# First stage of a hybrid attention and convolution backbone: x and context loaded feature-major, the row factor applied when products leave PSUM, and attention values computed with tokens on partitions and kept in DRAM

## The chip, the cores and the metric

The kernel runs on one core of a Trainium2 chip. The metric is the device time of one execution in microseconds. Five engines work side by side, each on its own list of instructions: TensorE (PE) multiplies matrices into PSUM, VectorE (DVE), ScalarE (ACT) and GpSimd (POOL) work element by element, and SyncE (SP) mostly issues DMA transfers. An instruction that needs another engine's result waits on a semaphore, and everything behind it on its engine waits with it.

## What is computed

Two layers over 1024 latent tokens of 1024 features, with a context of 256 tokens. The change touches the first layer's input side:

```python
h_lat = rmsnorm(x, norm_g[0]) * (1 + scale) + shift       # scale, shift from c
h_ctx = rmsnorm(ctx, norm_g[0]) * (1 + scale_c) + shift_c # from c_ctx
...
proj = h_lat @ w_in
q = apply_rope(split_heads(proj[..., :q_end], N_Q_HEADS), cos, sin)
k = apply_rope(split_heads(proj[..., q_end:k_end], N_KV_HEADS), cos, sin)
v = split_heads(proj[..., k_end:v_end], N_KV_HEADS)
z = proj[..., v_end:]
...
kv_c = h_ctx @ w_in[:, q_end:v_end]
kc = split_heads(kv_c[..., :KV_WIDTH], N_KV_HEADS)
vc = split_heads(kv_c[..., KV_WIDTH:], N_KV_HEADS)
...
o = windowed_attention(q, k, v, kc, vc, sink)
y = (o * jax.nn.silu(z)) @ w_out
```

There are 16 query heads in 4 groups, each group with one key and one value head of 128. A query sees a window of 384 latent keys and all 256 context keys. The second layer is a gated convolution; nothing of it changes.

## The kernel before

Every fp32 operand is split into a high and a low part (fp32r), and each product of matrices is done as three: high by high, low by high, high by low. In the names the high part of the features is `hh` (`Hh`), the low part `hl` (`Hl`); for weights `whi` and `wlo`. Features stand on partitions in eight tiles (kt 0 to 7) of 1024 tokens. The splits of one tile are an ACT copy and a DVE or POOL subtraction.

*First stage.* The rows of x come with tokens on partitions (`xs0`, four tiles for tokens 0 to 511). ACT sums their squares, DVE makes the row factor, and PE turns the rows: the first ten by a product with a diagonal of factors (`dg`), the others by transposes of rows already scaled (`turn_scaled` at L455, `turn`, `turn_apart`). ACT and DVE then add scale and shift (`x_tile`). The modulation itself is made column block by column block: `ada_mm` (L400) multiplies silu(c) and silu(c_ctx) by the modulation weights, 32 columns at a time on four quarters of the array, and `ada_cols` turns the rows to columns. K, Q and V of group 0 and head 0 are accumulated over the eight tiles for the first 512 tokens (`x_mm`, L502, with `acc0`), and then for the other 512 (`acc1`), whose x comes feature-major from the host (`k_xt`) and is multiplied by a broadcast of the row factor (`rb1`). Context tiles (`c_tile`, L492) are turned on PE in between. V is computed feature-major like K; `vt_split` (L628) turns it with PE transposes of `vf` and splits it. `spin` is a product on zeros that keeps PE running.

*Attention.* A loop runs over 16 heads and 8 query blocks of 128. Each step issues the next block's scores, then `fill(FILL)` (L1319) takes 12 products (15 in a few steps) from a queue of projections that later heads need (q, z), then a product with values (`pv`, twice or so per head), then the transposes of the probabilities that DVE, ACT and POOL made meanwhile. At a change of group ("regroup") the key job and the value job (`job`, L1056) of the next group run whole. Weights come in a stream of 40 chunks (`wsA`), the first four split with DVE and the others with POOL.

PE's list is kept in program order (`pin("P")`); in the first stage DVE's and ACT's as well. Otherwise a scheduler orders DVE, ACT and POOL, with `tc.high_priority` and `after` (an order without a wait) as hints. SP issues all loads in order, each gated by one some eight loads earlier.

## Time and profile before

| | us |
|---|---|
| median of three runs | 1678.78 (1678.36 to 1679.4) |
| profiled execution | 1678.26 |
| its span | 1676.5 |
| PE busy | 1665.9 |
| DVE, ACT, POOL busy | 1116.2, 879.7, 868.1 |
| first product on x starts | 16.04 |
| first transposes of probabilities start | 82.7 |

The span runs from the first to the last instruction. "Busy" counts the time in which at least one instruction of the engine runs. The recorded duration of a product includes its way through the array, and products overlap: one with 512 columns is recorded with some 390 ns, while the next starts after 227. Steps are therefore read from start to start. The first stage ends and the attention begins around 70 to 80 us.

### The profile page before, as it was taken

The page shows a single profiled execution, that of the slowest core. Times are in us where ns is not written, and L with a number is a line of the kernel's source. Part 1 is how long each engine was busy: PE and PEld are TensorE (multiplying, and loading weights), DVE is VectorE, ACT ScalarE, POOL GpSimd, SP SyncE. Part 2 cuts the span into 40 slices and gives each one's busy share as a digit, 9 for nine tenths or more (in the row PEclk, how much of TensorE's full clock was granted, in tenths as well). Part 3 has the DMA queues.
Part 4 walks back from the last instruction along what each step waited for, and adds up shares of the span by engine and source line. Part 5 has one row for each costly group of instructions (what it writes and reads, how often), then busy time and mean ns, then how long its engine had stood idle before and what let it go on. Part 6 is the DMA issues. An engine that isn't in the chain of part 4 may idle for free.

```text
span 1676.5 us, 23887 instructions
## 1 busy us (share of the span) xinstructions
PE 1665.9 (99%) x8414; PEld 1409.6 (84%) x8414; DVE 1116.2 (67%) x2121; ACT 879.7 (52%) x1555; POOL 868.1 (52%) x720
## 2 busy tenths in 40 slices
PE   9999999999999999999999999999999999999998
PEld 6888888888888888888888888888888888888886
DVE  5755644556366645566234399999999999868732
ACT  6745544555355544555333365655656664556741
POOL 0256653666366663642001267999898887130400
PEclk9999999999999999999999999999999999999999
DMA  9434433545254443447976523020211212377881
GB/s 377 162 88 151 144 113 101 151 154 145 77 154 154 144 131 93 139 148 276 310 246 210 200 88 101 0 78 16 71 51 51 89 38 70 132 271 253 308 298 50
DMA packets 114935, 244.54 MB, mean 146 GB/s; under 512 B 11768, under 2 KB 36736, under 8 KB 114816
## 3 DMA queue, kind: packets, MB, share of 16 engines
q1 hardware_dynamic: 108736, 233.06, 41.3%
q10 hardware_dynamic: 6080, 9.97, 2.4%
q8 instruction: 66, 1.08, 0.3%
q14 instruction: 53, 0.43, 0.1%
HBM read 190.80 MB, written 41.69 MB: 139 GB/s over the span
## 4 chain that ended last, share of the span: by engine, by line
PE 98%; DMA 1%; DVE 0%; POOL 0%; SPq 0%; ACT 0%; issue 0%
PE psg L89 51%; PE pss L89 26%; PE pso L89 21%; DMA wraw_page<-in_k_win_dram 1%; SPq L89 0%; POOL rope_half L89 0%; DVE x_page L89 0%; POOL ql_page L89 0%; POOL low_page L89 0%; DVE wlo_page L89 0%; ACT whi_page L89 0%; DVE ptlo L89 0%; POOL p_page L89 0%; ACT pthi L89 0%; DVE hf_page L89 0%
## 5 line engine op out<-in xcount | busy, mean ns | idle before, releaser
L89 POOL TENSOR_TENSOR odd_half<-odd_half,prod_half 128x513 f32<-128x513 f32 (+2 forms) x252 | 314.4, 1256 | 24.4 <-ACT prod_half L89 10.8
L89 POOL TENSOR_TENSOR wlo_page<-wraw_page,whi_page 128x512 fp32r<-128x512 f32 (+1 forms) x104 | 172.0, 1669 | 181.8 <-DVE ql_page L89 71.6
L89 PE MATMUL psg<-hh_page,whi_page 128*128 128x512 f32 x600 | 236.2, 394 | 0.0
L89 PE MATMUL psg<-hl_page,whi_page 128*128 128x512 f32 x600 | 234.4, 391 | 0.0
L89 PE MATMUL psg<-hh_page,wlo_page 128*128 128x512 f32 x600 | 234.3, 390 | 0.0
L89 ACT ACTIVATE prod_half<-ubuf,dww 128x513 f32<-128x513 f32 (+2 forms) x252 | 165.7, 675 | 117.0 <-POOL odd_half L89 113.0
L89 PE MATMUL psg<-h2h_page,whi_page 128*128 128x512 f32 x464 | 181.9, 392 | 0.0
L89 PE MATMUL psg<-h2h_page,wlo_page 128*128 128x512 f32 x464 | 180.6, 389 | 0.0
L89 PE MATMUL psg<-h2l_page,whi_page 128*128 128x512 f32 x464 | 180.5, 389 | 0.0
L89 POOL TENSOR_SCALAR p_page<-p_page,sc 128x640 f32<-128x640 f32 (+1 forms) x128 | 99.7, 779 | 153.7 <-DVE sc L89 131.6
L89 DVE SCALAR_TENSOR_TENSOR pss<-ubuf,dww,pss 128x512 f32<-128x512 f32 (+3 forms) x270 | 172.9, 674 | 0.1
L89 DVE SCALAR_TENSOR_TENSOR pss<-ubuf,wsum,pss 128x512 f32<-128x512 f32 (+3 forms) x270 | 172.2, 674 | 0.2
L89 ACT ACTIVATE p_page<-p_page,sc 128x641 f32<-128x641 f32 (+1 forms) x128 | 103.1, 805 | 101.9 <-DVE sc L89 99.3
L89 DVE TENSOR_TENSOR ptlo<-pss,pthi 128x512 fp32r<-128x512 f32 (+2 forms) x144 | 102.0, 717 | 67.1 <-ACT pthi L89 66.0
L89 ACT ACTIVATE pthi<-pss 128x512 fp32r<-128x512 f32 (+2 forms) x144 | 87.4, 618 | 105.3 <-PE pss L89 99.4
L89 PEld LDWEIGHTS psg<-hh_page,wlo_page 128*128 128x128 f32 x600 | 112.7, 188 | 24.4
L89 PEld LDWEIGHTS psg<-hh_page,whi_page 128*128 128x128 f32 x600 | 112.7, 188 | 19.1 <-ACT hh_page L89 0.3
L89 PEld LDWEIGHTS psg<-hl_page,whi_page 128*128 128x128 f32 x600 | 112.8, 188 | 18.4
L89 ACT ACTIVATE whi_page<-wraw_page 128x1024 fp32r<-128x1024 f32 x88 | 92.6, 1053 | 51.6 <-PE psg L89 20.6
L89 PE MATMUL pso<-h2h_page,whi_page 128*128 128x512 f32 x304 | 118.3, 389 | 0.0
L89 PE MATMUL pso<-h2l_page,whi_page 128*128 128x512 f32 x304 | 118.3, 389 | 0.0
L89 PE MATMUL pso<-h2h_page,wlo_page 128*128 128x512 f32 x304 | 118.3, 389 | 0.0
(260 smaller groups left out, 3985.1 us busy)
## 6 DMA issues: line engine op xcount, KB each, us to landing
wraw_page<-in_k_wconv_dram SPq DMA_DIRECT2D x48, 512.0 KB, 3.4
wraw_page<-in_k_win_dram SPq DMA_DIRECT2D x40, 512.0 KB, 3.6
wo_page<-in_attn_w_out_dram SPq DMA_DIRECT2D x32, 512.0 KB, 6.4
wol_page<-wolA SPq DMA_DIRECT2D x32, 512.0 KB, 6.6
wo_page<-in_conv_w_out_dram SPq DMA_DIRECT2D x32, 512.0 KB, 7.0
wol_page<-wolC SPq DMA_DIRECT2D x32, 512.0 KB, 5.6
rope_half<-rope_half ACTq DMA_DIRECT2D x76, 128.0 KB, 2.4
araw_page<-in_k_ada_dram SPq DMA_DIRECT2D x16, 512.0 KB, 10.2
```

Of the source, the lines that this page charges most:

```text
L89: r = f(*a, **k)
```

## The change

x and ctx come from the host feature-major, all tokens (`k_xt`, eight tiles, and `k_ct`, two). A tile is multiplied by its scale column alone and split (`u_tile`: `uh`, `ul`). K and Q of group 0 and head 0, and now also Z of head 0, are accumulated from these for all 1024 tokens; Z runs five tiles late (`ZLAG`). The row factor is put in when the sum leaves PSUM (`scaled`). The sums of squares that it needs are made feature-major: ACT squares, POOL adds, and PE sums over partitions in `roots`; `spread` broadcasts the factor. What the shift adds to each output column is a sum over features of weight times shift: POOL multiplies and adds (`shift_part`), PE sums over partitions, and ACT adds it (`wb`).

The tiles `hh` and `hl` are then made from x, row factor, scale and shift (`h_tile`), and the context's from `ct` (`ctx_tiles`). Values are computed for all four groups at once with tokens on partitions (`v_block`: 24 products of 512 columns for each of 8 latent and 2 context blocks, with weights `wv` from the host), split, written to DRAM (`vd`), and read back for each group (`load_values`). So the value jobs, `vf` and `vt_split` go. K and Q of the first group get their positions on whole pages, with SP swapping the halves.

In the loop the number of fill products is 12, 12, 11, 10 for heads 0 to 3 and then 10 or 11, and 12 in the last head; at a change of group 54 products of the queue stand in place of the value job. `tie` puts POOL's weight splits behind a softmax operation. The stream has 36 chunks, of which DVE splits only the first.

```diff
+ZLAG = 5
+AT_ONCE = (7,)
+FILLED = 7
+PACE = (12, 12, 11, 10)
+POOLED = (2, 5)
...
-    wsA = WStream(chunks, nraw=4, lo_eng=lambda i: V if i < 4 else G)
+    wsA = WStream(chunks, nraw=2, lo_eng=lambda i: G if i else V)
...
+    def u_tile(kt, a, b):
+
+        if kt not in U:
+            U[kt] = pg.alloc(F32R, [1024], "uh"), pg.alloc(F32R, [1024], "ul")
+        h, l = (t[:, a:b] for t in U[kt])
+        g = mods[kt][:, 1, 0:1]
+        act(h, xt[kt][:, a:b], AF.Copy, scale=g)
+        stt(l, xt[kt][:, a:b], g, h.bitcast(F32), ALU.mult, ALU.subtract)
...
+        act(t, xt[kt], AF.Square)
+        tt(G, sqs, sqs, t, ALU.add)
...
+    def roots(sq, n, o):
+
+        for b in range(n):
+            PE.matmul(o[:, b:b + 1], sq[:, b * P:b * P + P], ones[:, 0:1], start=True, stop=True)
...
+    def shift_part(kts):
+
+        for kt in kts:
+            for i, n in enumerate("kqz"):
+                a, w, b = wb_pg[:, i * P:i * P + P], W0[n][0][:, kt], mods[kt][:, 0, 0:1]
+                t = a if kt == 0 else wb_pg[:, 3 * P:4 * P]
+                G.tensor_scalar(out=t, in0=w, scalar1=b, scalar2=1.0, op0=ALU.mult, op1=ALU.mult)
+                if kt:
+                    tt(G, a, a, t, ALU.add)
...
+                stt(f[:, 0:CT], ct[kt // 4][:, kt % 4], m[:, 1, 1:2], rbc, ALU.mult, ALU.mult)
+                act(h, f[:, 0:CT], AF.Identity, bias=m[:, 0, 1:2])
+                ctx_low.append(stt(l, f[:, 0:CT], m[:, 0, 1:2], h.bitcast(F32), ALU.add, ALU.subtract))
...
+            r1 = roots(sqs, 8, ps_o(1))
+            pg.free(sqs)
+            rc = roots(csq[0][:, 0], 2, ps_o(1))
...
+    spread(rc, 2, rbc)
+    for kt in range(ZLAG, KT - 1):
+        x_mm(kt, "z")
+    spread(r1, 8, rb)
+    ctx_tiles(range(KT))
+    x_mm(KT - 1, "z")
...
+        behind_ctx(stt(f, xt[kt], m[:, 1, 0:1], rb, ALU.mult, ALU.mult))
+        act(Hh[kt], f, AF.Identity, bias=m[:, 0, 0:1])
+        if kt in POOLED:
+            act(f, f, AF.Identity, bias=m[:, 0, 0:1])
+            for a in range(0, 1024, 512):
+                split_lo(G, *(t[:, a:a + 512] for t in (Hl[kt], f, Hh[kt])))
+        else:
+            stt(Hl[kt], f, m[:, 0, 0:1], Hh[kt].bitcast(F32), ALU.add, ALU.subtract)
...
+    run(v_block(oc, TB))
+    h_tile(0)
+    h_tile(1)
+    vz = scaled(acc0["z"])
+    oc = ps_o(0)
+    run(v_block(oc, TB + 1))
...
+    V.tensor_copy(wb, o[:, 0:3])
...
     for kt in range(KT):
+        for n in range(4):
+            run(v_mm(accv[n], kt, *v_lhs(kt, n)))
         if kt + 2 < KT:
+            h_tile(kt + 2)
...
+            fill(FILL if h == NH - 1 else PACE[h] if h < 4 else 10 + (qb % 3 == 0))
...
+        if h and h % 4 == 0 and qb == 2:
+            load_values(h // 4)
...
-            run(job(("v", g)))
+            enqueue(("z", nxt[0]))
+            fill(54)
```

PE's first instructions before, behind 32 spins, where `zerr` are the zeros of `spin`, `araw` the modulation weights, and `dg` the diagonal of row factors:

```order
L89 MATMUL pso_233<-araw_page_99,c_page_170 32x256 x4
L89 MATMUL pso_233<-araw_page_100,c_page_170 32x256 x4
L89 MATMUL psg_247<-dg_half_212,x_page_90 128x128
L89 MATMUL psg_247<-dg_half_212,x_page_91 128x128
L89 MATMUL psg_247<-dg_half_212,x_page_92 128x128
L89 MATMUL pso_251<-ident,arow_half_98 128x2 x2
L89 MATMUL psg_247<-dg_half_212,x_page_93 128x128
L89 MATMUL psg_257<-dg_half_212,x_page_90 128x128
L89 MATMUL psg_257<-dg_half_212,x_page_91 128x128
L89 MATMUL psg_257<-dg_half_212,x_page_92 128x128
L89 MATMUL psg_257<-dg_half_212,x_page_93 128x128
L89 MATMUL pss_85<-zerr_page_82 128x512 x2
```

PE's first instructions in the changed kernel:

```order
L94 MATMUL pss_85<-zerr_page_82 128x512 x8
L94 MATMUL pso_171<-araw_page_96,c_page_159 32x128 x8
L94 MATMUL pss_85<-zerr_page_82 128x512 x2
L94 MATMUL pso_184<-ident,arow_half_180 128x2
L94 MATMUL pss_85<-zerr_page_82 128x512 x4
L94 MATMUL pss_168<-uh_page_191,whi_page_195 128x512
L94 MATMUL pss_168<-ul_page_192,whi_page_195 128x512
L94 MATMUL pss_168<-uh_page_191,wlo_page_196 128x512
L94 MATMUL pss_168<-uh_page_191,whi_page_195 128x512
L94 MATMUL pss_168<-ul_page_192,whi_page_195 128x512
L94 MATMUL pss_168<-uh_page_191,wlo_page_196 128x512
```

The turning of x stands no longer ahead of the first products, one modulation block stands there instead of two half blocks of double width, and 14 spins instead of 34.

POOL, whose first instruction of work before is a weight split of the attention, starts in the changed kernel with ten sums of squares (`sqs`, `csq`) and the 45 instructions of `shift_part`, 24 products and 21 sums.

DVE in the changed kernel, where the context tiles are made (`hcf` and `hcl`; `own` are the sums that leave PSUM):

```order
L94 SCALAR_TENSOR_TENSOR hcf_half_696<-ct_page_136,mod,rbc_half_646 128x256
L94 SCALAR_TENSOR_TENSOR hcl_page_677<-hcf_half_682,mod,hch_page_676 128x256
L94 SCALAR_TENSOR_TENSOR hcf_half_704<-ct_page_136,mod,rbc_half_646 128x256
L94 SCALAR_TENSOR_TENSOR hcf_half_708<-ct_page_136,mod,rbc_half_646 128x256
L94 SCALAR_TENSOR_TENSOR hcf_half_700<-ct_page_136,mod,rbc_half_646 128x256
L94 SCALAR_TENSOR_TENSOR hcl_page_695<-hcf_half_696,mod,hch_page_694 128x256
L94 SCALAR_TENSOR_TENSOR hcl_page_695<-hcf_half_704,mod,hch_page_694 128x256
L94 SCALAR_TENSOR_TENSOR hcl_page_695<-hcf_half_708,mod,hch_page_694 128x256
L94 SCALAR_TENSOR_TENSOR hcl_page_695<-hcf_half_700,mod,hch_page_694 128x256
L94 TENSOR_TENSOR own_page_812<-pss_168,rb_page_647 128x512
L94 TENSOR_TENSOR own_page_815<-pss_169,rb_page_647 128x512
L94 TENSOR_TENSOR own_page_812<-pss_168,rb_page_647 128x512
```

Before, `hcl` stood in pairs between the feature tiles of the second 512 tokens:

```order
L89 TENSOR_TENSOR hcl_page_661<-hf_page_665,hch_page_660 128x256
L89 TENSOR_TENSOR hcl_page_661<-hf_page_672,hch_page_660 128x256
L89 SCALAR_TENSOR_TENSOR hl_page_409<-hf_page_651,mod_177,hh_page_408 128x512
L89 SCALAR_TENSOR_TENSOR hf_page_687<-xt_page_162,mod_178,rb_page_514 128x512
L89 TENSOR_TENSOR hcl_page_661<-hf_page_692,hch_page_660 128x256
L89 TENSOR_TENSOR hcl_page_661<-hf_page_699,hch_page_660 128x256
```

The sixteen operations of the context tiles now stand together, ahead of the evacuation of the first products and of all feature tiles.

DVE in the changed kernel, further on: the fourth feature tile's low part is `hl_page_940`:

```order
L94 SCALAR_TENSOR_TENSOR hf_page_959<-xt_page_120,mod,rb_page_647 128x1024
L94 COPY ident<-pso_891 128x3
L94 TENSOR_TENSOR vout_page_887<-pso_862,vout_page_887 128x512
L94 TENSOR_SCALAR pso_1199<-dww_raw,cs 128x256
L94 SCALAR_TENSOR_TENSOR hf_page_941<-xt_page_118,mod,rb_page_647 128x1024
L94 SCALAR_TENSOR_TENSOR hl_page_958<-hf_page_959,mod,hh_page_957 128x1024
L94 SCALAR_TENSOR_TENSOR pso_1199<-ident,abt,pso_1199 128x128
L94 SCALAR_TENSOR_TENSOR hf_page_977<-xt_page_124,mod,rb_page_647 128x1024
L94 SCALAR_TENSOR_TENSOR hf_page_997<-xt_page_130,mod,rb_page_647 128x1024
L94 SCALAR_TENSOR_TENSOR pso_1199<-ident,abt,pso_1199 128x128
L94 TENSOR_TENSOR own_page_812<-own_page_812,cos_page_733 128x1024
L94 SCALAR_TENSOR_TENSOR hl_page_940<-hf_page_941,mod,hh_page_939 128x1024
```

It stands behind the `hf` of three later tiles, the copy of `wb` and the multiplication of K by the cosines.

717 lines of the change are left out of this document (334 added, 383 removed).

## The prediction

> **What bounds the kernel now.** I read the page's busy table and its chain first, then TensorE's waits, the busy times by stretch, and last the timelines of TensorE and of the DVE (VectorE) and POOL (GpSimd) engines.
>
> ```profile
> span 1676.5 us, 23887 instructions
> PE 1665.9 (99%) x8414; PEld 1409.6 (84%) x8414; DVE 1116.2 (67%) x2121; ACT 879.7 (52%) x1555; POOL 868.1 (52%) x720
> PE 98%; DMA 1%; DVE 0%; POOL 0%; SPq 0%; ACT 0%; issue 0%
> PE pss L89 <- DVE zerr_page L89: 2.0, 1, 2.0
> PE pso L89 <- DMA araw_page<-in_k_ada_dram: 0.6, 1, 0.6
> 0.00:20.00 20.00, 17.14 (x101) 12.57 (x101) 7.39 (x22) 14.09 (x22) 1.12 (x7) 1.00 0.89 344
> 20.00:40.00 20.00, 20.00 (x159) 13.25 (x159) 12.65 (x28) 10.75 (x17) 0.00 (x0) 1.00 1.03 408
> ```
>
> PE is busy for 1665.9 of 1676.5 us and is 98% of the chain that ended last; its two longest waits are 2.0 and 0.6 us. So the time is what PE streams, plus its start and end. An edit pays only if it takes work off PE, and it costs only where it makes PE wait. The stretches (span, then PE, PEld, DVE, ACT, POOL busy, clock, DMA) show POOL at work for 1.12 us in the first 20 us and for none in the next 20, while DMA runs at 408 GB/s. That idle POOL is what the change fills.
>
> The profiled execution took 1678.26 us, its span and 1.76 us around it; the median is 1678.78, 0.5 us away. The sum is made against 1678.26.
>
> **PE work that goes.** The step of a product with 512 columns, and the price of a transpose, are read from starts, since durations overlap:
>
> ```profile
> 53.00 0.39 PE L89 MATMUL pss<-hl_page,whi_page 128*128 128x512 f32 x1
> 53.23 0.60 PE L89 MATMUL pso<-ident,x_page 128*128 128x128 f32 x4
> 53.59 0.47 PE L89 MATMUL psg<-hh_page,whi_page 128*128 128x512 f32 x1
> 53.90 0.39 PE L89 MATMUL psg<-hh_page,wlo_page 128*128 128x512 f32 x1
> 66.01 0.28 PE L89 MATMUL psg<-hch_page,wlo_page 128*128 128x256 f32 x1
> 66.13 0.28 PE L89 MATMUL psg<-hch_page,whi_page 128*128 128x256 f32 x1
> ```
>
> From 53.00 to 53.23 a product takes 0.23 us. Four transposes move the next start from 53.23 to 53.59, and the product behind them takes 0.31 instead of 0.23: (0.36 + 0.08) / 4 = 0.11 us each. A product with 256 columns takes 0.12, a little over half of 0.227.
>
> ```profile
> L89 PE MATMUL psg<-ident,x_page x24: 272/273/329, 18.9 to 58.6; 128*128 128x128 f32 x24
> L89 PE MATMUL pso<-ident,x_page x14: 270/272/273, 44.0 to 61.1; 128*128 128x128 f32 x14
> L89 PE MATMUL psg<-dg_half,x_page 128*128 128x128 f32 x20 | 2.9, 284 | 0.0
> L89 PE MATMUL pso<-ident,vf_half x40: 270/272/273, 65.3 to 638.9; 128*128 128x128 f32 x40
> L89 PE MATMUL pso<-ident,r 128*128 128x128 f32 x8 | 1.1, 274 | 0.0
> ```
>
> - x and ctx come feature-major: 24 + 14 transposes and 20 records of scaled ones go, 58 x 0.11 = **6.4 us**.
> - Values are computed with tokens on partitions: the 40 transposes of `vf` go, 40 x 0.11 = **4.4 us**.
> - Context values become 48 products of 512 columns instead of 96 of 256: 48 x (0.24 - 0.227) = **0.6 us**.
>
> All the other products of 512 columns are the same in number.
>
> **The start.** The columns are start, duration, engine, line, operation:
>
> ```profile
> 1.98 9.49 PE L89 MATMUL pss<-zerr_page 128*128 128x512 f32 x32 [1.98 <-DVE zerr_page L89]
> 12.67 0.64 PE L89 MATMUL pso<-araw_page,c_page 128*32 128x256 f32 x8 [0.55 <-DMA araw_page<-in_k_ada_dram]
> 13.24 0.94 PE L89 MATMUL psg<-dg_half,x_page 128*128 128x128 f32 x6
> 15.50 0.70 PE L89 MATMUL pss<-zerr_page 128*128 128x512 f32 x2
> 16.04 0.40 PE L89 MATMUL pss<-hh_page,whi_page 128*128 128x512 f32 x1
> 16.37 1.07 PE L89 MATMUL pso<-araw_page,c_page 128*32 128x256 f32 x16
> ```
>
> The first product on x stands at 16.04, of which 1.2 us is modulation, 0.4 its columns (4 records of 0.11) and 1.8 turning x (16, counted above): 12.6 us of nothing useful, two groups of spins among it. In the changed kernel it needs the third 512 KB load. The sixth landed at 12.6 (the row at 12.67 ends a wait for it), and at 408 GB/s each takes 1.28, so the third lands at 8.8; splits into high and low parts (below) add 1.9, so 10.7. Less 0.8 of modulation that is 9.9, a gain of 2.7, of which the loads of the q and z weights (fifth and seventh, 11.3 and 13.9) can take some back. I take **2.0**, bounds 0 and 2.7.
>
> **PE work that comes.** Sums of squares and the shift's contribution are 13 one-column products in full fp32, two records each; no such row exists here. The nearest is `r`: 8 records from 41.1 to 41.8 us in the first stage, 0.10 to 0.11 a record, though with 128 columns. So 26 x 0.11 = **2.9 us** (0 to 2.9). Spreading the row factors takes six products more, 12 x 0.11 = **1.3**. The modulation runs as 256 records of half the width in place of 128 that step by 1.07 / 16 = 0.067. If the price goes by width it is nothing more; if by record, 128 x 0.067 = 8.6 us. I take **1.0**, near the lower end, since a record's matrix is only 32 columns wide.
>
> Sum without waits: -6.4 - 4.4 - 0.6 - 2.0 + 2.9 + 1.3 + 1.0 = **-8.2 us**.
>
> **New waits.** POOL now adds squares (7 of 1024 elements, then three shorter), and then 24 products and 21 sums of 128 elements for the shift, while DVE makes the low parts next to it.
>
> ```profile
> L89 POOL TENSOR_TENSOR wlo_page<-wraw_page,whi_page 128x1024 fp32r<-128x1024 f32 x32 | 78.9, 2468 | 65.8 <-ACT whi_page L89 34.8 <-DMA wraw_page<-in_k_wconv_dram 29.2 <-PE psg L89 1.7
> L89 POOL TENSOR_SCALAR p_page<-p_page,sc 128x640 f32<-128x640 f32 x96 | 77.5, 807 | 127.4 <-DVE sc L89 105.5 <-PE pss L89 16.6 <-PE pso L89 3.0
> L89 POOL TENSOR_SCALAR p_page<-p_page,sc 128x512 f32<-128x512 f32 x32 | 22.2, 694 | 26.3 <-DVE sc L89 26.2
> L89 POOL TENSOR_TENSOR low_page<-low_page,lhi_page 128x512 f32<-128x512 f32 x64 | 83.0, 1297 | 37.6 <-ACT lhi_page L89 20.6 <-ACT p_page L89 16.7
> L89 POOL TENSOR_TENSOR odd_half<-odd_half,prod_half 128x265 f32<-128x265 f32 x28 | 21.6, 781 | 4.7 <-ACT prod_half L89 3.3 <-POOL odd_half L89 0.3
> L89 DVE TENSOR_TENSOR hcl_page<-hf_page,hch_page 128x256 fp32r<-128x256 f32 x8 | 3.3, 422 | 0.2
> L89 DVE SCALAR_TENSOR_TENSOR hl_page<-hf_page,mod,hh_page 128x512 fp32r<-128x512 f32 x8 | 6.0, 749 | 0.9 <-ACT hh_page L89 0.8
> ```
>
> The squares are 7 x 2.47 = 17 us of POOL. By the slopes of the next rows (0.807 to 0.694 over 128 elements; 1.297 to 0.781 over 247), a 128-wide product is estimated at 0.36 and a sum at 0.50, so the shift takes 24 x 0.36 + 21 x 0.50 = 19 us. What that does to DVE is shown late in the kernel:
>
> ```profile
> 1570.43 0.69 DVE L89 TENSOR_TENSOR v_page<-v_page,zsl_half 128x512 f32<-128x512 f32 x1 [2.93 <-DMA zsl_half<-zsd]
> 1571.04 4.09 DVE L89 TENSOR_TENSOR gs_page<-v_page,gs_page 128x512 fp32r<-128x512 f32 x3
> 1571.21 3.37 POOL L89 TENSOR_TENSOR v_page<-v_page,zsl_half 128x512 f32<-128x512 f32 x2 [4.87 <-ACT woh_page L89]
> ```
>
> DVE's operation alone takes 0.69 us. With POOL running, three take 4.09 and POOL's two 3.37 in place of 2 x 1.3: with two operands in SBUF the two engines take turns.
>
> The Trainium skill ("SBUF — State Buffer", section "Who interferes with whom") states that such an operation and a GpSimd one that reads SBUF hold their shared port exclusively, the loser waiting in full. These rows agree; by that rule the change would come out as in the second rival.
>
> - *Context tiles.* Count from R, the end of `roots` on PE. Before the context's factor is spread stand 24 products (5.5), 64 modulation records (2.6 to 4.3) and columns (1.8): R + 10; with the copy R + 11. DVE then has 16 operations of 0.42: R + 17.7. Behind the spread PE has 18 products and 16 records more, so it starts on the context keys at R + 16.2, and needs tile 7 seven times 3 x 0.12 later, R + 18.7. Alone, nothing waits. In turns, each of the 16 also pays one POOL operation, 0.42 on average: R + 24.4, a wait of 5.7. The shift stands beside them for its whole length, since its second half needs shifts that PE makes at R + 9.5. I take **3.5** of 0 to 5.7: the rows shown had two full queues, POOL's here waits for itself between operations.
> - *The fourth feature tile's low part* stands on DVE behind 24 operations (own pages, seven `hf`, outputs, a multiplication by cos), some 21.7 us from the last context tile by these rows, and PE wants it 20.2 us after that tile (0.4 + two value blocks of 24 x 0.227 + 0.7 + 36 x 0.227): 1.5 us late. With POOL's low halves of tiles 2 and 5 beside it, and the shift that `wb` waits for, up to 4.5. Queued behind `wb` on PE is all the rest. I take **1.8** (0 to 4.5).
> - *First stage.* `ul` of 1024 elements beside the square sums: 0.8, bounds 0 and 2.0. POOL is in step with ACT there, so most turns fall in slack.
> - *Attention.* Two rows show a short margin:
>
> ```profile
> 172.15 1.17 POOL L89 TENSOR_SCALAR p_page<-p_page,sc 128x640 f32<-128x640 f32 x1 [5.91 <-DVE sc L89]
> 174.03 0.71 PE L89 MATMUL pss<-ident,p_page 128*128 128x128 f32 x5
> ```
>
> POOL ends the softmax at 173.32 and PE takes it at 174.03, 0.71 later. From head 4 a step fills in 10 or 11 products instead of 12, 1.6 x 0.227 = 0.37 us shorter, 0.74 over the two steps that a softmax has. Only such steps can wait. I take **0.6** (0 to 3).
>
> The values' way over DRAM, 10 stores and the loads per group, costs no PE time as long as it lies beside products (first group: at least two steps of 4 us; later ones are asked for at qb 2 and have a step to come in). Without that cover a round trip of two transfers would show, some 3 us. Moving low parts of weights from DVE to POOL, the rope on full pages and fewer spins also hide behind products.
>
> Sum of waits: 3.5 + 1.8 + 0.8 + 0.6 = 6.7. So -8.2 + 6.7 = -1.5: 1678.26 - 1.5 = **1676.8 us**.
>
> **Rivals.**
> 1. *Nothing waits.* For it: every tile is ready before PE by the rows taken alone, bar one. Against: the rows at 1571. 1678.26 - 8.2 = 1670.0; with the lower ends of start and modulation 1668.5.
> 2. *DVE and POOL take turns all along* (slower). One mechanism at the context tiles and the feature tiles: 5.7 + 4.5 + 2.0 + 0.6 = 12.8, so +4.6: 1682.9. From waits of 8.2 + 3.4 = 11.6 us on it decides. For it: the turns are strict where shown. Against: PE's own waits give DVE time back.
> 3. *Shorter fills starve the softmax.* If every fourth of the 96 steps from head 4 on waits 0.37, that is 8.9 instead of 0.6: 1685.1. Against: it takes margins under 0.74 us in a quarter of the steps, and the one shown is the shortest of its head.
> 4. *It doesn't do what it says:* the values come late from DRAM, or the turns that go were hidden. A chain that is 98% PE speaks against the second; the first gives 1676.8 + 3 = 1679.8.
>
> **How the numbers follow.** About 0.2%, 3.4 us, is what a measurement of this kernel can tell from no change. Forecast 0.44, its own range 1672 to 1680 (faster 0.14, same 0.27, slower 0.03); nothing waits 0.26 (faster); turns 0.20 (slower 0.16, same 0.04); starved 0.07 (slower 0.05, same 0.02); late values 0.03 (same). Faster 0.40, same 0.36, slower 0.24. The range runs from rival 1's low end to just past rival 2: 1668.5 to 1683.5; what is above it (modulation priced by record, starving) holds under 0.1, what lies below as much.
>
> **What would show it.** No `vf` and no x transposes on PE; the first `uh` product near 10.7 us; waits of PE for `hcl` and for `hl` in the first 100 us, several us with POOL's `wacc` beside them, or none (rival 1); DVE's `hcf` and `hcl` near 0.42 or near 0.84 us; modulation steps of 0.035 or 0.067 us; PE waiting for `p_page` (rival 3) or for `vh` (rival 4). The prediction is wrong if PE's loss sits in a place not named here, or if the 128-wide POOL operations are far from their estimate.

## The result, and the profile after

| | before | after |
|---|---|---|
| median of four runs, us | 1679.03 (1678.36 to 1679.4) | 1694.34 (1691.49 to 1696.47) |
| ratio to before | | 1.0091, 95% interval 1.0073 to 1.0108 |
| profiled execution, us | 1678.26 | 1696.47 |
| its span, us | 1676.5 | 1694.7 |

The change makes the kernel slower, by 15.3 us at the median and by 18.2 us between the two profiled spans. The forecast was 1676.8 us, some 1.5 us faster, with a range up to 1683.5. The profiled execution is the slowest of the four, 1.6 to 5.0 us above the others, and the account below is of that one.

The page of the changed kernel's profile first: span, busy times, and the chain of work that ended last.

```profile
span 1694.7 us, 23950 instructions
PE 1664.7 (98%) x8414; PEld 1404.8 (83%) x8414; DVE 1137.8 (67%) x2121; ACT 877.7 (52%) x1523; POOL 910.1 (54%) x765
PE 88%; POOL 4%; DMA 3%; issue 2%; DVE 1%; ACT 1%; SPq 0%; ACTq 0%; POOLq 0%; DVEq 0%
```

PE's share of the chain falls from 98% to 88%. Its busy time is only 1.2 us lower, although transposes went, because a slow clock and longer records behind each pause fill it again. Next come PE's waits in the changed kernel: what was waited for, us in all, times, longest.

```profile
PE pss L94 <- POOL p_page L94: 4.5, 3, 2.0
PE pso L94 <- DVE vout_page L94: 3.5, 1, 3.5
PE pso L94 <- DMA vh_page<-vd: 2.2, 2, 1.1
PE pss L94 <- DVE zerr_page L94: 2.0, 1, 2.0
PE pss L94 <- ACT uh_page L94: 1.8, 1, 1.8
PE pso L94 <- DVE hcl_page L94: 1.7, 2, 1.1
PE psg L94 <- DVE wlo_page L94: 1.6, 1, 1.6
PE psg L94 <- POOL wlo_page L94: 1.1, 1, 1.1
PE psg L94 <- DVE zs_page L94: 1.1, 1, 1.1
PE psg L94 <- DVE rope_half L94: 0.8, 1, 0.8
PE pss L94 <- DVE sc L94: 0.7, 1, 0.7
PE pso L94 <- DVE r L94: 0.4, 1, 0.4
PE pss L94 <- DVE ul_page L94: 0.4, 2, 0.3
PE pso L94 <- DVE ms L94: 0.4, 1, 0.4
```

Before, this view had three rows, 2.0, 0.6 and 0.3. It now has fourteen, most of them one or two waits at one place; no single engine has become the bound. The stretches of the changed kernel (span, then PE, PEld, DVE, ACT and POOL busy, PE's clock, DMA's share and rate) show where they lie:

```profile
0.00:20.00 20.00, 14.32 (x76) 9.21 (x80) 9.46 (x18) 11.06 (x17) 3.48 (x8) 0.91 0.89 340
20.00:40.00 20.00, 20.00 (x164) 15.03 (x160) 9.28 (x16) 12.17 (x14) 13.93 (x6) 1.00 1.03 409
80.00:100.00 20.00, 16.54 (x62) 13.24 (x61) 19.41 (x21) 11.44 (x11) 10.31 (x8) 0.83 0.45 132
330.00:520.00 190.00, 185.75 (x1040) 161.87 (x1039) 106.41 (x244) 97.50 (x208) 116.86 (x105) 1.00 0.47 146
```

POOL is at work from the start now, 13.93 of the second 20 us, without harm to PE there. From 80 to 100 us PE idles for 3.46 us, and its clock stands at 0.83. In the attention it idles for 4.25 us from 330 to 520. That stretch in the kernel before:

```profile
330.00:520.00 190.00, 189.88 (x1061) 165.91 (x1060) 105.69 (x233) 94.12 (x202) 110.93 (x100) 1.00 0.43 131
```

There PE idled for 0.12 us. POOL is busy for 62% of this stretch after and 58% before: it is not short of throughput, but late at single moments.

**The account of the profiled run.** For every record on PE I took the distance from its start to the next start, and summed it by tile in both kernels.

| part of the sum | forecast, us | measured, us |
|---|---|---|
| turns of x (`x`, `dg`) | -6.4 | -5.9 |
| turns of `vf` | -4.4 | -3.4 |
| context values | -0.6 | -0.5 |
| start (spins and the waits behind them) | -2.0 | -2.5 |
| one-column products | +2.9 | +3.7 |
| spreads of the factors | +1.3 | +1.2 |
| modulation and its columns | +1.0 | -0.9 |
| sum | -8.2 | -8.3 |
| waits and slow clock behind other products | +6.7 | +25.5 |

With about 1 us in the rest, these make the 18.2. What PE streams came out as forecast in the sum, though not term by term; the waits did not. Of the 25.5 us, the waits above give 18.4 (their sum of 22.2 less the 2.0 for `zerr` and the 1.8 for `uh`, which stand behind spins). A slow clock gives an estimated 5.6 in three places shown below. The first product behind a pause takes some 0.1 us longer (0.50 against 0.40 in the rows at 18.69 and 16.67 below), 17 times. That is 25.7; with estimates and rounded waits in it, such a sum is good to a microsecond or two.

**Start.** TensorE's list at the start of the changed kernel (start, duration, operation, the wait before it):

```profile
10.70 0.72 PE L94 MATMUL pss<-uh_page,whi_page 128*128 128x512 f32 x1 [1.81 <-ACT uh_page L94]
...
12.70 0.63 PE L94 MATMUL pss<-uh_page,whi_page 128*128 128x512 f32 x1
13.13 0.63 PE L94 MATMUL pss<-ul_page,whi_page 128*128 128x512 f32 x1
...
16.67 0.40 PE L94 MATMUL psg<-ul_page,whi_page 128*128 128x512 f32 x1
18.69 0.50 PE L94 MATMUL psg<-uh_page,wlo_page 128*128 128x512 f32 x1 [1.62 <-DVE wlo_page L94]
```

The first product on x stands at 10.70, as worked out; in the profiles of the experiments it stands between 9.92 and 11.01. The steps behind it are 0.43 instead of 0.23, at a slow clock after the pause of 1.81 us. In e8, with the same four spins but a pause of 0.25, they are 0.23, and so they are in e3 and e12 with twelve spins. The six products up to the next group of records at 14.12 take 3.42 us with a wait of 0.26 (`ul`) among them; in e12 the same six take 2.34 with a wait of 0.48, so the slow clock costs 1.3 us here. And at 18.69 PE waits for the low part of Z's weights, which DVE made here:

```profile
16.25 2.38 DVE L94 TENSOR_TENSOR wlo_page<-wraw_page,whi_page 128x256 fp32r<-128x256 f32 x1 [1.10 <-ACT whi_page L94]
```

The same operation takes 0.43 with POOL at rest (a row of e12, below). This one stood beside POOL's first addition of squares, from 16.00 to 18.36.

**End of the first stage.** The first and last instructions of the shift on POOL, with three of its middle:

```profile
52.82 2.46 POOL L94 TENSOR_SCALAR wacc_half<-wraw_page,mod 128x128 f32<-128x128 f32 x4 [5.16 <-DVE mod L94]
...
64.22 0.43 POOL L94 TENSOR_SCALAR wacc_half<-wraw_page,mod 128x128 f32<-128x128 f32 x1
64.73 0.51 POOL L94 TENSOR_TENSOR wacc_half<-wacc_half 128x128 f32<-128x128 f32 x1
65.33 0.42 POOL L94 TENSOR_SCALAR wacc_half<-wraw_page,mod 128x128 f32<-128x128 f32 x1
...
82.20 1.55 POOL L94 TENSOR_TENSOR wacc_half<-wacc_half 128x128 f32<-128x128 f32 x1
```

The shift runs from 52.82 to 83.75, 31 us where 19 were estimated. A product and a sum take 0.43 + 0.51, near the 0.36 + 0.50 of the estimate, but with the gap behind each the pair moves by 1.11, and several operations take 1.2 to 2.5 where DVE works beside them. What that does to DVE and PE:

```profile
79.27 1.29 DVE L94 TENSOR_TENSOR own_page<-psg,rb_page 128x512 f32<-128x512 f32 x2 [3.99 <-POOL wacc_half L94]
84.76 0.68 DVE L94 TENSOR_TENSOR vout_page<-pso,vout_page 128x512 fp32r<-128x512 f32 x1
```

```profile
85.58 1.12 PE L94 MATMUL pso<-ones,wacc_half 128*128 128x1 f32 x6 [3.46 <-DVE vout_page L94]
86.56 0.77 PE L94 MATMUL pss<-wvhi_page,hh_page 128*128 128x512 f32 x1
87.14 0.63 PE L94 MATMUL pss<-wvlo_page,hh_page 128*128 128x512 f32 x1
...
92.68 0.42 PE L94 MATMUL pss<-wvhi_page,hl_page 128*128 128x512 f32 x1
```

DVE waits for POOL for 3.99 us ahead of `own`, which asks nothing of the shift: its page was one of the raw weights that the shift still reads. Everything behind it on DVE is late, the values' low part (`vout`) among it, and PE stands for 3.46 us. Then its clock falls: 14 products from 86.56 to 92.68 take 6.12 us, 2.9 more than at 0.227 each. Not all of this is lost in every run. In the profiles of e4, e6, e8, e12 and e14, with nearly the same pause (2.91 to 3.44), only six to nine products are slow, and PE waits 1.4 us further on for the low part of the last feature tile. So a part of the 2.9 stands where PE would have waited anyway.

**Attention.** One of the waits for the softmax, on POOL and on PE:

```profile
376.99 1.27 POOL L94 TENSOR_TENSOR rope_half<-rope_half,sin_page 128x512 f32<-128x512 f32 x1 [3.27 <-DMA rope_half<-rope_half]
378.24 0.69 POOL L94 TENSOR_SCALAR p_page<-p_page,sc 128x512 f32<-128x512 f32 x1
```

```profile
378.99 0.65 PE L94 MATMUL pss<-ident,p_page 128*128 128x128 f32 x4 [1.34 <-POOL p_page L94]
```

POOL idles for 3.27 us before a multiplication by the sine whose input comes by DMA, does it, and only then the softmax that PE waits for. The softmax stands behind it in POOL's list. The wait at 556.28 is of the same kind (2.14 us on POOL for the DMA). The longest, 1.99 us at 692.45, has the sine and two more operations of POOL ahead of the softmax, and a slow clock behind it: seven products take 2.96 us, 1.4 more than at 0.227 each.

```profile
693.98 0.63 PE L94 MATMUL psg<-hl_page,whi_page 128*128 128x512 f32 x1
...
696.94 0.40 PE L94 MATMUL psg<-hh_page,wlo_page 128*128 128x512 f32 x1
```

### The profile page after: what moved, and what is told of

It is laid out like the page before. It is cut to its first block, busy times and chain, and to the rows that moved or that the text cites. A ratio compares the mean times of both kernels' runs of the same rounds, so it can differ in the third digit from the quotient of the medians.

```text
span 1694.7 us, 23950 instructions
## 1 busy us (share of the span) xinstructions
PE 1664.7 (98%) x8414; PEld 1404.8 (83%) x8414; DVE 1137.8 (67%) x2121; ACT 877.7 (52%) x1523; POOL 910.1 (54%) x765
## 4 chain that ended last, share of the span: by engine, by line
PE 88%; POOL 4%; DMA 3%; issue 2%; DVE 1%; ACT 1%; SPq 0%; ACTq 0%; POOLq 0%; DVEq 0%
PE psg L94 44%; PE pss L94 24%; PE pso L94 20%; POOL wacc_half L94 2%; DMA rope_half<-rope_half 1%; POOL wlo_page L94 1%; DMA vh_page<-vd 1%; POOL rope_half L94 1%; DMA wolC<-low_page 0%; DMA wo_page<-in_conv_w_out_dram 0%; DMA wo_page<-in_attn_w_out_dram 0%; DMA wraw_page<-in_k_win_dram 0%; POOL low_page L94 0%; POOL csq_page L94 0%; POOL p_page L94 0%
## 5 line engine op out<-in xcount | busy, mean ns | idle before, releaser
L94 PE MATMUL psg<-hh_page,wlo_page 128*128 128x512 f32 x528 | 207.4, 393 | 1.1 <-POOL wlo_page L94 1.1
L94 PE MATMUL psg<-hh_page,whi_page 128*128 128x512 f32 x528 | 207.0, 392 | 0.0
L94 PE MATMUL psg<-hl_page,whi_page 128*128 128x512 f32 x528 | 206.9, 392 | 0.0
L94 POOL TENSOR_TENSOR wlo_page<-wraw_page,whi_page 128x512 fp32r<-128x512 f32 (+1 forms) x96 | 160.4, 1686 | 73.8 <-ACT whi_page L94 65.1
L94 ACT ACTIVATE whi_page<-wraw_page 128x1024 fp32r<-128x1024 f32 (+1 forms) x87 | 88.8, 1024 | 64.0 <-PE psg L94 21.3
L94 DVE CUSTOM_DVE_ANT_0 p_page<-pss,mask_page,nsink 128x640 f32<-128x640 f32 (+1 forms) x112 | 96.4, 860 | 30.3 <-PE pss L94 25.5
L94 PEld LDWEIGHTS psg<-hh_page,wlo_page 128*128 128x128 f32 x528 | 99.6, 189 | 20.0 <-POOL wlo_page L94 1.5
L94 PEld LDWEIGHTS psg<-hl_page,whi_page 128*128 128x128 f32 x528 | 99.6, 189 | 17.8
```

The costliest lines, as they stand in the source:

```text
L94: r = f(*a, **k)
```

## The experiments

All are edits of the changed kernel. The kernel before, run beside them, took 1678.5 to 1679.5 us. Times are medians (with their range), ratios are to before. The four runs of the changed kernel reach from 1691.49 to 1696.47 us, so a median that differs from its 1694.34 by 2 us or less shows no change by itself.

### The shift and the end of the first stage

**e1_shift_one** sums the shift's contribution over one feature tile of eight; the other seven are left out of the result.

```diff
-    shift_part(range(KT))
+    shift_part(range(1))
```

> GpSimd multiplies and adds the shift's contribution for the first feature tile only (3 operations instead of 45), so the contribution of the other seven tiles is left out. Theory (GpSimd's shift is what PE waits for): the waits of PE for hcl (1.7 us in two) and the 3.5 us ahead of the wacc products go, and with the pause the 15 products at 0.43 us a step behind it (3.0 us too long): about 8 us less than the changed kernel, near 1686. DVE's hcf and hcl near 0.42 us. Rival (DVE's own queue is what is late, GpSimd only stands beside it): at least 3 us of the wait for vout stay, and under 4 us are gained.

Measured: 1687.31 us (1683.78 to 1689.52), ratio 1.0046 (1.0031 to 1.0060), 7.0 less than the changed kernel. The stretch in question:

```profile
80.00:100.00 20.00, 20.00 (x93) 16.68 (x92) 16.95 (x19) 10.61 (x11) 3.34 (x3) 1.00 0.39 106
```

PE idles no more there and its clock is full; the waits for `hcl` and `vout` are gone (1.7 + 3.5, and 2.9 of clock). So the shift on POOL, with all that its length makes late, is what PE pays for at this place, some 7 us of the 15.

**e2_wb_later** leaves the shift as it is and has PE take it later, so that the list no longer stops for it.

```diff
-    o = ps_o(1)
-    for i in range(3):
-        PE.matmul(o[:, i:i + 1], wb_pg[:, i * P:i * P + P], ones[:, 0:1], start=True, stop=True)
...
     sa, sb = ps_s(), ps_s()
...
             run(v_mm(accv[n], kt, *v_lhs(kt, n)))
+        if kt == 1:
+            o = ps_o(1)
+            for i in range(3):
+                PE.matmul(o[:, i:i + 1], wb_pg[:, i * P:i * P + P], ones[:, 0:1], start=True, stop=True)
...
```

> The three wacc products on PE, and all that hangs on them, are issued behind the value products of the first two feature tiles (48 products) instead of ahead of them. Theory (the pause of 3.5 us at the wacc products makes the clock fall, and 15 products run at half speed): the wait shrinks to what the first feature tile needs, under 1.5 us, the products behind it step by 0.227, 4 to 6.5 us gained, near 1688 to 1690. Rival (the slow products have another cause than the pause): they stay slow, and at most 3.5 us are gained. Second rival (the keys of the first group come later and the attention waits): nothing is gained, since a wait of some us appears ahead of the first scores.

Measured: 1692.12 us (1690.96 to 1693.84), ratio 1.0080 (1.0065 to 1.0095): 2.2 less, with ranges that overlap. The long wait and the slow clock go, but not the lateness:

```profile
PE pss L94 <- DVE hl_page L94: 1.7, 2, 1.1
...
PE pss L94 <- ACT hh_page L94: 1.0, 1, 1.0
```

PE now waits for the feature tiles behind, which DVE makes late as before.

**e13_pages_apart** keeps the raw weights' pages until the values are done, so that `own` gets another page.

```diff
     for n in "kqz":
-        pg.free(*W0[n])
+        pg.free(*W0[n][1:])
...
     pg.free(rb)
+    for n in "kqz":
+        pg.free(W0[n][0])
```

> The pages of the raw weights, which GpSimd reads for the shift to the end, are given back behind the value products of the eight tiles, so that no DVE output takes their place. Theory (DVE's evacuation of z waits 4.0 us for GpSimd because it writes into such a page, and all of DVE's list, with it the turn that PE needs for the wacc products, is late by that): DVE's wait for wacc goes, PE's wait ahead of the wacc products falls from 3.5 to about 2 us (what the shift itself needs, it ended at 83.75 and PE stood from 81.97), the clock does not fall or less long, 1.5 to 4.5 us gained, near 1691. Rival (GpSimd's shift alone sets it): the wait stays above 3 us and the time is the same within 1 us.

Measured: 1705.15 us (1703.06 to 1706.58), ratio 1.0154 (1.0139 to 1.0170): 10.8 more. DVE's operation on `own` has no wait in front of it now:

```profile
76.02 1.27 DVE L94 TENSOR_TENSOR own_page<-psg,rb_page 128x512 f32<-128x512 f32 x2
```

So the page that was used again is shown as what held DVE. It is not what cost PE its time, for PE's waits of this kernel read:

```profile
PE pss L94 <- ACT hh_page L94: 4.4, 1, 4.4
PE pso L94 <- POOL wacc_half L94: 3.8, 3, 1.8
```

POOL's shift is late by itself: beside a DVE that no longer stands still it ends at 88.03 in place of 83.75, and PE waits for it three times, by up to 1.84 us at once. The feature tiles come late as well. DVE makes the `hf` that the wait of 4.4 us hangs on at 104.13, behind the positions of K and Q and a wait of 6.47 us for the DMA that swaps their halves. That this order comes from the pages that are still held is likely, and not shown.

**e9_shift_act** gives the shift's 24 products to ACT and leaves POOL the sums.

```diff
...
-                t = a if kt == 0 else wb_pg[:, 3 * P:4 * P]
-                G.tensor_scalar(out=t, in0=w, scalar1=b, scalar2=1.0, op0=ALU.mult, op1=ALU.mult)
+                j = (3 * kt + i) % 8
+                t = a if kt == 0 else tmp[:, j * P:j * P + P]
+                act(t, w, AF.Copy, scale=b)
...
```

> ScalarE makes the 24 products of the shift and GpSimd only the 21 sums; everything is computed. GpSimd's part falls from some 31 us in the changed kernel to 21 x 0.46 to 0.56, 12 us. Theory (GpSimd's shift ends too late): it ends ahead of PE's context products, the waits for hcl, for wacc's turn and the slow products behind it go, 6 to 7 us gained, near 1688. Rival (ScalarE's high parts of the context tiles now stand behind products that wait for GpSimd): the wait for hch takes their place and under 3 us are gained.

Measured: 1698.59 us (1696.12 to 1699.02), ratio 1.0118 (1.0101 to 1.0135): 4.3 more. POOL's part shrinks to 11.4 us, but ACT makes the context's high parts late (a wait of 1.8 for `hch`), and DVE's list, put in another order by the scheduler, has PE wait 4.3 us for `hl`.

**e5_shift_on_pe** sums the shift on PE, with the raw weights and the shift's column in full fp32, and takes POOL out of it.

```diff
...
+        o = ps_o(1)
+        for i, n in enumerate("kqz"):
+            for kt in range(KT):
+                PE.matmul(o[:, i:i + 1], W0[n][0][:, kt], mods[kt][:, 0, 0:1], start=kt == 0, stop=kt == KT - 1)
...
     spread(r1, 8, rb)
+    shift_part()
...
```

> The shift's contribution is made by 24 fp32 products with one column on PE (48 records) ahead of the last z products of the first stage, instead of 45 operations on GpSimd and three products; everything is computed. Theory (GpSimd's shift costs PE 8 us of waits and slow clock, as its removal showed 7): 48 x 0.11 = 5.3 us more streaming less the 0.7 of the three products, so 1689 to 1692, with no wait for wacc's successors and no slow stretch behind 80 us. Rival (one-column records step far below 0.11 us): 1686 to 1688.

Measured: 1700.98 us (1694.98 to 1701.88), ratio 1.0125 (1.0106 to 1.0144): 6.6 more. TensorE's list there:

```profile
68.52 7.35 PE L94 MATMUL pso<-mod,wraw_page 128*128 128x1 f32 x48 [0.69 <-ACT rb_page L94]
75.73 0.77 PE L94 MATMUL psg<-uh_page,whi_page 128*128 128x512 f32 x1
76.31 0.63 PE L94 MATMUL psg<-ul_page,whi_page 128*128 128x512 f32 x1
76.73 0.63 PE L94 MATMUL psg<-uh_page,wlo_page 128*128 128x512 f32 x1
```

The 48 records take 7.2 us, 0.15 each. The products behind them step by 0.42, the slow clock, though PE stood only for the 0.69 us ahead of the records. By the median that is dearer than POOL's late shift: 13.7 us more than e1, where most of the shift is left out. Not all of it is the records' own, since in this profile the clock reads 0.66 already from 50 to 60 us, ahead of them, where the changed kernel's reads 1.00.

### The start

**e3_spins** runs twelve spins in place of four ahead of the first product on x.

```diff
-    spin(4)
+    spin(12)
```

> Twelve instead of four products on zeros ahead of the first product on x. Theory (the start is bounded by the split weights of z, which PE waits for at 18.7 us): the first six products step by 0.23 instead of 0.43, PE waits longer at the z weights, and the time is the same within 1 us. Rival (the slow clock at the start is lost time): 2 us less.

Measured: 1694.22 us (1693.00 to 1695.78), ratio 1.0092 (1.0077 to 1.0107): no change. The clock is full in the first 20 us, and the wait for Z's low part moved. It was expected to grow, but takes 1.64 us as before (1.62), and ends at 17.16 instead of 18.69. DVE made that low part sooner too (at 14.72 instead of 16.25), again beside POOL, because ACT's and DVE's lists wait for a product of PE ahead of it (until 13.32 instead of 14.86). Whether the spins did this is not shown: in the profiles with four spins the same wait ends anywhere from 16.92 (e1) to 19.10 (e2). In this profile the clock then reads 0.68 from 50 to 60 us, where the changed kernel's reads 1.00.

**e12_start** has the spins, and starts the sum of squares two tiles later and in another order, so that POOL rests while DVE makes Z's low part.

```diff
-        if kt == 0:
+        if kt == 2:
             act(sqs, xt[kt], AF.Square)
...
-        for k in {2: (0, 1), 3: (2, 3), 4: (4, 5, 6), 5: (7,)}.get(kt, ()):
+        for k in {2: (2, 0), 3: (1, 3), 4: (4, 5, 6), 5: (7,)}.get(kt, ()):
```

> The first sums of squares on GpSimd start with the third feature tile, and twelve products on zeros stand ahead of the first product on x. Theory (DVE's low part of the z weights stands behind GpSimd's first sum, 2.4 us instead of 0.43, and PE waits 1.6 us for it): that wait goes and the clock is at 1.00 in the first 20 us, 2 to 4 us gained, near 1691. Rival (PE waits there for the z weights themselves): the wait stays and the time is the same.

Measured: 1693.04 us (1692.66 to 1693.16), ratio 1.0083 (1.0068 to 1.0099): 1.3 less, within the changed kernel's own range. DVE's list in this kernel:

```profile
15.14 0.43 DVE L94 TENSOR_TENSOR wlo_page<-wraw_page,whi_page 128x256 fp32r<-128x256 f32 x1 [1.11 <-ACT whi_page L94]
```

0.43 us in place of 2.38, and PE's wait is gone. In e3, with the spins alone, the operation took 2.38 as well, so POOL beside it was the cause. The product that waited at 18.69 starts at 15.81 now, 2.9 us sooner: the 1.6 of the wait and the 1.3 of slow clock. Of this 1.3 is left in the median; in this profile the clock reads 0.89 from 40 to 50 us and 0.94 from 50 to 60, where it was full in the changed kernel.

**e11_roots_twice** adds 16 one-column products ahead of the roots, 32 records in all; their result is not used.

```diff
+            for b in range(16):
+                PE.matmul(o2[:, b:b + 1], sqs[:, b % 8 * P:b % 8 * P + P], ones[:, 0:1], start=True, stop=True)
```

> 16 more one-column products (32 records) ahead of the sums of squares on PE; their result is overwritten. Theory (a stretch of one-column products is taken by the clock gate for a pause, since the clock fell to 0.66 in the ten microseconds behind it in three profiles of nine): 32 x 0.11 = 3.5 us for the records, and the clock falls behind them in the profile, 2 to 3 us more at half speed: 5 to 7 us slower than the changed kernel, near 1700. Rival (the falls there are chance or come from real pauses): 3.5 us slower and a clock of 1.00 from 50 to 60 us.

Measured: 1699.38 us (1696.32 to 1700.57), ratio 1.0119 (1.0104 to 1.0134): 5.0 more, with this stretch:

```profile
50.00:60.00 10.00, 9.65 (x44) 8.69 (x44) 6.30 (x18) 3.25 (x5) 1.30 (x2) 0.60 0.10 28
```

PE is busy for 9.65 of 10 us, and its clock is 0.60. At 0.12 a record (16 took 1.95 us in the changed kernel) the 32 make 3.9 of the 5.0 us. That narrow products cost more than their own time is what the clock in this profile says; the runs spread too far to show it by their times.

### Attention

**e4_twelve** puts back 12 fill products in every step.

```diff
-            fill(FILL if h == NH - 1 else PACE[h] if h < 4 else 10 + (qb % 3 == 0))
+            fill(FILL)
```

> Twelve fill products in every step, as before, instead of 12, 12, 11, 10 and then 10 or 11. Theory (shorter steps leave the softmax too little time): PE's three waits for p_page, 4.5 us, go or halve, and 3 to 5 us are gained, if the queue lasts. Rival (GpSimd's order, with a rope operation ahead of the softmax, makes these waits): they stay, within 1 us; the queue runs dry ahead of the ends of heads, and the time is the same or some us more.

Measured: 1727.99 us (1722.62 to 1730.87), ratio 1.0289 (1.0267 to 1.0310): 34 more. The queue runs dry before its next job comes in (the three steps whose transposes start at 456, 459 and 463 us have no product of it), and PE's waits grow to 12.4 us for `sc` and 8.0 for `p_page`. The shorter steps are forced: the value job that stood at each change of group is done in the first stage, 54 products of the queue stand there now, and so fewer are left for the steps.

**e14_even_fill** gives the steps up to one product more each, and takes them from the 54 at a change of group.

```diff
-            fill(FILL if h == NH - 1 else PACE[h] if h < 4 else 10 + (qb % 3 == 0))
+            fill(FILL if h == NH - 1 else (12, 12, 12, 11)[h] if h < 4 else 11 + (qb % 3 == 0))
...
-            fill(54)
+            fill(24)
```

> 24 fill products at a change of group instead of 54, and 12, 12, 12, 11 and then 11 or 12 in the steps instead of 12, 12, 11, 10 and then 10 or 11; loads as in the changed kernel. Theory (fill products of the steps were moved to the change of group, where the value job had stood, and the shorter steps leave the softmax too little): the three waits for p_page (4.5 us) halve or go, and waits at the change of group, where the new keys come, take some of it back: 1 to 4 us gained. Rival (the steps' length does not matter, GpSimd's order does): p_page stays near 4.5 us, and the change of group costs 3 us or more: 1697 or above.

Measured: 1709.12 us (1706.71 to 1711.12), ratio 1.0178 (1.0163 to 1.0194): 14.8 more.

```profile
PE pss L94 <- ACT qh_page L94: 9.8, 3, 3.6
...
PE pss L94 <- POOL p_page L94: 1.8, 2, 1.0
```

With longer steps the three waits for the softmax at their old places are gone, and 1.8 us is waited for it elsewhere in place of 4.5, so the steps' length is part of that wait. But three times, ahead of the last head of a group (at 415.04, 596.71 and 776.95), PE waits more than 3 us for that head's q. At 415.04 the last two products of the queue stand right before the wait; that the queue is late there because 30 products fewer were taken at the change of group is argued.

**e8_loads_early** asks for a group's values one step earlier, and does the product with values that stood in the way earlier too.

```diff
-        if h and h % 4 == 0 and qb == 2:
+        if h and h % 4 == 0 and qb == 1:
             load_values(h // 4)
...
-        if qb == 1 and h and h % 2 == 0:
+        if qb == (h % 4 == 2) and h and h % 2 == 0:
```

> At a change of group the last value products of the old group are issued one step earlier, and the new group's values are read from DRAM one step (4 us) earlier. Theory (the transfers are asked for some 1 us too late): PE's two waits for vh, 2.2 us, go, 1 to 2.2 us gained. Rival (the transfers are slow because of their 512-byte pieces, and hold up what is issued behind them): the waits for vh go, but the time is the same, since waits for weights or probabilities come in their place.

Measured: 1689.96 us (1689.37 to 1691.33), ratio 1.0068 (1.0053 to 1.0083): 4.4 less, more than the waits for `vh` alone (2.2). They are gone, and `p_page` falls from 4.5 to 2.7, while `sc` rises from 0.7 to 3.0. All waits in the attention together fall from 10.4 to 6.2, which agrees with the time. Why more fell than those for `vh` is not shown.

**e7_no_tie** lets POOL's weight splits take any place.

```diff
     def tie(ins):
-        if anchor_p:
-            after(ins, anchor_p)
+        pass
```

> The weight splits on GpSimd are no longer ordered behind a softmax operation. Theory (the order is not what makes the waits, except the 1.1 us for a weight's low part): that wait goes, waits for p_page come or grow, within 3 us of 1694. Rival (the order delays weights all along the attention): 3 to 8 us less.

Measured: 1701.61 us (1699.33 to 1704.15), ratio 1.0132 (1.0115 to 1.0149): 7.3 more, and `p_page` is waited for 11.9 us. The order of POOL's list decides about the softmax, and the tie earns its place.

**e6_rope_behind** ties the sine's multiplication in the same way.

```diff
-            tt(G, w, w, sin[:, sl], ALU.mult)
+            (tie if hold is None else lambda i: i)(tt(G, w, w, sin[:, sl], ALU.mult))
```

> GpSimd's multiplication by the sines, which waits for the swap of halves by DMA, is ordered behind the softmax operation that was issued last, as the weight splits are. Theory (PE's three waits for p_page, 4.5 us, come from GpSimd standing in that wait with the softmax operation behind it): they go, 3 to 4.5 us gained, near 1690. Rival (the shorter steps leave too little time whatever GpSimd's order): the waits stay within 1 us.

Measured: 1694.22 us (1690.08 to 1696.31), ratio 1.0089 (1.0074 to 1.0105). The order at the three waits did not change, since the tie holds only to the softmax before; this run tells nothing.

**e10_sine_dve** moves that multiplication from POOL to DVE.

```diff
-            tt(G, w, w, sin[:, sl], ALU.mult)
+            tt(V if hold is None else G, w, w, sin[:, sl], ALU.mult)
```

> DVE in place of GpSimd multiplies the queries' swapped halves by the sines. Theory (GpSimd standing in the wait for the swap's DMA, with the softmax operation behind it, makes PE's waits for p_page): these go, 4 us gained, near 1690. Rival (any engine that stands in that wait has softmax work behind it): the waits go over to sc or ptlo, which DVE makes, and the time is the same or worse.

Measured: 1698.86 us (1695.28 to 1699.56), ratio 1.0114 (1.0099 to 1.0129): 4.5 more. The waits for `p_page` fall to 0.9 us, so the sine in front of the softmax was the main cause of them. But:

```profile
PE pso L94 <- DMA vh_page<-vd: 4.8, 2, 2.4
```

PE comes sooner to the values and to POOL's low parts of weights (1.8, from 1.1) and waits there for 3.3 us more, nearly the 3.6 that were won. Behind the wait of 1.8 its clock falls too. Where the rest of the 4.5 lies is not settled; in this profile the clock reads 0.71 from 50 to 60 us.

### Together

**e15_together** joins e8, e12, e13 and the spins.

> Earlier loads of values, later sums of squares, twelve spins, and the raw weights' pages kept, together. If the parts add up: 1694.3 - 4.4 - 1.3 - 1.5 to 4.5, so 1684 to 1687, still slower than the kernel before (1678.8): the streaming that is saved, 8 us, is below the waits that stay in the first stage (hcl, hl, wacc) and the attention (p_page and weights). Rival (the parts hang on the same waits): 1688 to 1690.

Measured: 1698.55 us (1696.17 to 1700.47), ratio 1.0113 (1.0096 to 1.0130): 4.2 more. This held e13's pages, so it could not tell whether the other parts add.

**e16_three_parts** joins e2, e8 and e12, without the pages.

> The edits of e2 (shift taken in later), e8 (values asked for a step earlier) and e12 (squares in another order, twelve spins), without the pages kept apart that were in e15. Theory (each of the three removes waits of its own, at places far from each other: start of the first stage, its end, attention; what spoiled e15 was the pages): the gains add, 2.2 + 4.4 + 1.3 = 7.9 us less than 1694.3, so some 1686.5 (1685 to 1688.5); TensorE's waits above its pitch fall to some 5 in the first 60 us or less, 7 from there to the first scores, and 21 in the loop. Rival (waits inside the first stage move to the next thing that is late, so e2 and e12 do not add): 1690 us, as e8 alone, with the first stage's part as large as in after. Either way slower than the kernel before, 1679.

Measured: 1685.65 us (1685.07 to 1688.69), ratio 1.0047 (1.0032 to 1.0061): 8.7 less than the changed kernel, against 7.9 for the three apart and 4.4 for e8, the largest of them. With ranges of 0.5 to 5 us on each the sum is not shown to a microsecond, but the profile shows each part at its own place: the waits for Z's low part (e12), for `vout` (e2) and for `vh` (e8) are all gone, and what came in their place is much as in the single runs (`hl` 1.1 and `hh` 1.0, `sc` 2.5). So these are separate waits at separate places. It is the best of the versions that compute everything, and still 6.2 us slower than before. No version beat the kernel before.

## Why the prediction was wrong

**What held.** The work on PE: -8.2 forecast, -8.3 measured, with the first `uh` product at 10.70 as worked out. That the sums agree to 0.1 is luck. The modulation is priced by width and not by record, and came out 1.9 lower than taken; the transposes of `vf` gave 1.0 less than taken, and the one-column products cost 0.8 more. For these the prediction said that the kernel before has no row. It has one, `pso<-ones,qa_half`, 16 records late in the second layer that step by 0.10, about the price that was taken from `r`; behind the roots they stepped by 0.12, and six of the new ones stood at the slow clock.

**The step that failed** is the sum of waits, 3.5 + 1.8 + 0.8 + 0.6 = 6.7. The runs show 18.4 us of waits and some 5.6 of slow clock in its place, about half of it in the attention, which was put at 0.6:

| place | forecast, us (bounds) | measured, us |
|---|---|---|
| context tiles | 3.5 (0 to 5.7) | 1.7 |
| fourth tile's low part and `wb` | 1.8 (0 to 4.5) | 3.5, and 2.9 of slow clock |
| first stage | 0.8 (0 to 2.0) | 2.4, and 1.3 of slow clock |
| attention | 0.6 (0 to 3) | 10.4, and 1.4 of slow clock |
| second layer (`r`, at 1565.85) | none | 0.4 |

- *Context tiles.* The mechanism is there, the size half. DVE's operations on them took 0.56 (three in 1.69 us) instead of 0.42, not the 0.84 of strict turns:

```profile
63.22 1.69 DVE L94 SCALAR_TENSOR_TENSOR hcl_page<-hcf_half,mod,hch_page 128x256 fp32r<-128x256 f32 x3
```

- *Fourth tile and `wb`.* PE waited for no feature tile's low part in this profile. The wait came at `wb`, the other half of this term, and its root is the shift's length, mis-sized at 19 us for 31. The gap of 0.1 us behind each of the 45 operations, left out, makes some 4.5 of the difference; the rest is turns with DVE. On the way to PE it went through something that the working did not have, a page that the shift still reads; but e13 shows that without the page the shift holds PE as long. e1 shows some 7 us for the shift with all that follows, the 1.7 at the context tiles included. And a pause of 3.46 us has a second price, 2.9 us of slow clock in this profile, that no term held.
- *First stage.* The term was for `ul`, and PE waited 0.4 for it. The wait of 1.6 came at another low part, Z's: one turn between DVE and POOL, 2.38 for 0.43, fell on the one operation with no slack (e12). The waits alone pass the upper bound of 2.0, and the clock was left out.
- *Attention.* The largest error, 10.4 for 0.6. Three causes are shown: the softmax behind the sine's multiplication on POOL (e10: 4.5 to 0.9), steps shortened to 10 or 11 products (e14: 4.5 to 1.8; e4 shows that 12 cannot be fed), and values asked for too late (e8: 2.2 to 0). The last was rival 4's mechanism, to which I gave 0.03: the claim that a step covers the loads did not hold. The softmax was rival 3's in part, 8.9 us at 0.07; I read one margin of 0.71 us as the shortest and took the rest for longer. But rival 3 was many waits of 0.37 us, and what came is three of 1.2 to 2.0, more than the 0.74 that shorter steps take from a margin: the order of POOL's list, which no term held, makes up the difference. The remaining 3.7 us for weights, gates, positions and `sc` are places that the prediction did not name.

**The rivals.** "Nothing waits" is refuted, and late values alone were priced at 3. Turns between DVE and POOL (rival 2) decide at two places and not all along: at Z's low part, and by stretching POOL's shift. The outcome is parts of rivals 2, 3 and 4 at once. They were weighed as alternatives; e16 agrees with waits that add.

**What stays open.** The runs explain the waits at their places; what the attention would cost with the value jobs left in it, and only the first stage changed, was not tried. Nor is the rest of e8's gain settled, nor what of e10's loss is its own. With the best three edits together, 6.2 us over the kernel before remain, which is explained by the waits that are left and not by an experiment.

## What to carry to other kernels

When a kernel is 98% bound by one engine's stream, price not only the work that goes but the slack that it gave to others: value products and transposes were PE's work and at the same time the cover for softmax, weights and loads. Sum small waits over all places instead of choosing between them, and add to each pause of some 2 us or more what the clock may take afterwards. Before lending a page again, ask which slow queue still reads it.
